# Scores of attention group 0 in one piece over four PSUM banks, with later transposes and a later exchange of maxima

## The chip, the cores and the metric

The kernel runs on one core of a Trainium2 chip. The core has five engines with a queue each, and every engine works through its own queue strictly in the order in which the program issued to it: PE (TensorE, matrix products), DVE (VectorE), ACT (ScalarE), POOL (GpSimd) and SP (SyncE, which here only issues DMAs). Engines wait for each other through semaphores. PE writes its products to PSUM, which has eight banks of 128 x 512 fp32; a bank that still holds something to be read can't be written by the next product. The metric is the time of one execution on the device in microseconds (us).

## The reference

Two residual layers over a sequence of 512 rows of 1024 numbers, all in fp32. Layer 0 mixes tokens by attention over three groups (dilations 1, 4, 16), layer 1 by a short gated convolution; a squared-ReLU MLP follows each of them. The change concerns the attention only, cut here to what matters:

```python
def mixer_a(h, w_qkv, q_gain, k_gain, w_o, cos, sin):
    qkv = (h @ w_qkv).reshape(B, S, A_GROUPS, 3, A_HEADS, HEAD_DIM)      # 3 groups x (q, k, v) x 16 heads x 64
    for g in range(A_GROUPS):
        q = partial_rope(rms_norm(qkv[:, :, g, 0], q_gain[g]), cos, sin)
        k = partial_rope(rms_norm(qkv[:, :, g, 1], k_gain[g]), cos, sin)
        num, den, mx = dilated_group(q, k, qkv[:, :, g, 2], dil, radius) # scores, row max, exp, sums, scores @ v
    wts = jnp.exp(mx - jnp.max(mx, axis=0, keepdims=True))               # the groups are joined by their maxima
    num = jnp.sum(wts[..., None] * jnp.stack(nums, 0), axis=0)
    den = jnp.sum(wts * jnp.stack(dens, 0), axis=0)
    return (num / den[..., None]).reshape(B, S, D_MODEL) @ w_o
```

## The kernel before

Each fp32 factor is split into a high and a low part (`split`, L285: ACT casts the high part at L288, the low part is a subtraction at L289, by POOL for the weights), and each product is made of three PE matmuls: high by high, high by low, low by high.

**Units, blocks and groups.** The attention goes by pairs of heads, p = 0 to 7. A pair has three units of projections: A (q and k of group 0, q of group 1), B (k of group 1, q and k of group 2) and V (the values of all groups). A unit multiplies 8 weight tiles (a tile is one k of 128 rows) with 4 blocks r of 128 rows of the sequence, in 96 matmuls of 384 columns at L128, into the 4 banks of the pool psG, one bank for each r. It is cut into 4 blocks of 24 matmuls with 2 weight tiles each (pair 0's first unit into 8). Positions are counted in "groups" of 16 such matmuls, so a block is 1.5 groups long, one matmul is 0.0625 group and a pair is 18 groups. In a block the matmuls go by r, so a unit's first matmul needs the bank of r = 0 and its seventh that of r = 1. When a bank's last matmul is through, it is emptied: unit A by `evacA`, unit B by `evacB` (L320), unit V by `evacV` (L327), which casts the values with ACT at L291 and subtracts with DVE at L292. Only then can the next unit's matmuls write to that bank.

**The order written by hand.** Between the matmuls of the units stand the tasks of the attention. `PLACES` (L60) gives each task a position in groups after the end of unit A (for A's tasks) or unit B (for all others); its first entry is for pair 0, the second for pairs 1 to 6, the third for pair 7. `attn_tasks` (L587) puts them on a heap, and the loop at the end of the kernel runs a task when the matmul that reaches its position has been issued. Before the first matmul of each block the same loop calls `prep_to` and `load_to`, which prepare the two weight tiles of the block two blocks further on (ACT's cast and POOL's subtraction) and issue the DMAs of later tiles. There are 6 buffers for prepared tiles (wh and wl) and 4 for raw ones (wraw): a raw buffer is loaded again when POOL's subtraction L289 has read it, and SP, which issues the loads (L567, or L725 for the output weights), waits for that.

**The attention tasks of a pair** that the change and the prediction touch, with their places for pairs 1 to 6, in groups after the end of unit B, so within unit V:

- sqB (0.17 to 0.92): the four squares of the rows of B (ACT L361) and their sums (DVE L362); rsB (0.97): the reciprocal root in eleven small DVE instructions (L365, L151 to L157); mulB (1.07 to 1.43): scaling (DVE L371) and rotation (L376, L378), three of the four blocks on POOL.
- S0: the scores of group 0. `S0(bp)` does two of the four blocks b of queries. Each needs 3 matmuls for each of 2 heads, 64 rows of the array by 256 columns (L443), the two heads side by side on the two halves of the array. A call takes two banks of the pool psT (3 banks, tile "st"), and DVE then adds the mask and takes the row maximum, four times (L447). The first call stands at 0.45, the second at 1.0.
- E0: eight exponentials on ACT (L466), four from 1.1 and four from 1.65, in steps of 0.15.
- TA and TB, the transposes (`qk_fill`, L380): four PE transposes (L387) bring a q or k into a bank of psT, ACT scales and casts it (L401), DVE takes the low part (L403). TB fills k1, q2 and k2 at 4.05, 4.24 and 4.43. A fill of k1 or k2 is two instructions on ACT and two on DVE, one for each head.
- X1 (3.1) and X2 (5.3): the exchange of maxima; a spread on DVE (L424), eight small matmuls (L433) and a copy (L478).
- S12, E12, W, N12, N0 from 6.5 on: scores of groups 1 and 2, weights and normalization; then PT and PV: PT transposes the scores, PV multiplies them with the values into the one bank of the pool psO (tile "o"). The last PV of a head is followed by ACT's copy (L547) and DVE's sum (L548), which empty that bank. Pair 0's last PV stands at 0.61 of pair 1's counting, that of the other pairs at -0.12 of the next pair's.

After pair 7 follow the output projection (its first unit uses three of psG's banks), the MLP, the convolution and the second MLP, none of which the change touches.

Of the kernel before, what the change touches and what calls it, by code (L numbers as in the profile page):

```python
# [11 lines left out]
F32 = mybir.dt.float32  # L12
# [23 lines left out]
def _constants():  # L36
# [10 lines left out]
    for n, b in enumerate((0, 1, 3)):  # L47
# [11 lines left out]

PLACES = [  # L60
    dict(sqA=0.52, rsA=0.95, mulA=2.62, dmA=0.05, TA=7.6, dT=0.25, sqB=0.08, rsB=1.22, mulB=2.1, dmB=0.1, TB=6.2, S0=2.6,
         dS=1.0, E0=3.75, X=5.5, lX=2.0, S12=8.1, dS12=0.3, E12=8.7, dE12=0.2, W=10.3, lW=0.35, lF=0.9, N0=11.65, N12=10.75,
         dN=0.04, P=12.45, dP=0.58, gP=0.5, lP=1.6, qA=0, qB=0, pA=0, pB=3, pN=2, vA=0, vB=0, xq=2.7, dxq=0.3, xs=5.35,
         lg=2.48, dlg=0.36, tb=4.6, dtb=0.15, gc=6.7),
    dict(sqA=0.02, rsA=0.87, mulA=1.79, dmA=0.28, TA=4.8, dT=0.19, sqB=0.17, rsB=0.8, mulB=1.07, dmB=0.12, TB=4.05, S0=0.45,
         dS=0.55, E0=1.1, X=3.1, lX=2.2, S12=6.5, dS12=0.24, E12=7.1, dE12=0.2, W=8.9, lW=0.35, lF=0.9, N0=10.25, N12=9.4,
         dN=0.04, P=10.9, dP=0.64, gP=0.9, lP=1.6, qA=0, qB=0, pA=0, pB=3, pN=2, vA=0, vB=12),
    dict(sqA=0.02, rsA=0.87, mulA=1.79, dmA=0.28, TA=4.8, dT=0.19, sqB=0.17, rsB=0.8, mulB=1.07, dmB=0.12, TB=4.05, S0=0.45,
         dS=0.55, E0=1.1, X=3.1, lX=2.8, S12=6.8, dS12=0.24, E12=7.4, dE12=0.2, W=9.2, lW=0.4, lF=1.0, N0=10.7, N12=9.75,
         dN=0.04, P=12.0, dP=0.5, gP=0.45, lP=1.2, qA=0, qB=0, pA=0, pB=3, pN=2, vA=0, vB=9),  # L70
]

# [2 lines left out]
def trunk_kernel(ctx, tc, x, norm1, norm2, wqkv, qgain, kgain, wo, win, conv, wout, w1, w2, c_rope, c_m0, c_m12, out):  # L75
    nc = tc.nc
    pe, act, dve, pool, sync = nc.tensor, nc.scalar, nc.vector, nc.gpsimd, nc.sync
    ctx.enter_context(tc.manual_schedule())

    def ptile(p, shape, dt, name, **kw):  # L80
        return p.tile(shape, dt, name=name, **kw)
# [323 lines left out]
    def q0v(t, h, b):  # L405
        return t[64 * h:64 * h + 64, 128 * b:128 * b + 128]
# [26 lines left out]
            pe.matmul(ps[32 * b:32 * b + 32, :n], fold, t[:, n * b:n * b + n], start=True, stop=True)  # L433
        return ps[:, :n].rearrange("p (a j) -> p j a", a=4)

    def S0(bp):
        ps = [ptile(psT, [128, 512], F32, "st") for _ in range(2)]
        (qh, ql), (kh, kl) = qk["q0"], qk["k0"]
        for b2 in range(2):
            b = 2 * bp + b2  # L440
            for q, (a, k) in enumerate(((qh, kh), (qh, kl), (ql, kh))):
                for h in range(2):
                    pe.matmul(ps[h][:, 256 * b2:256 * b2 + 256], q0v(a, h, b), k0v(k, h, b), start=(q == 0), stop=(q == 2))  # L443
        for h in range(2):
            for b2 in range(2):
                b = 2 * bp + b2
                dve.tensor_tensor_reduce(out=sm0[:, h, b], in0=ps[h][:, 256 * b2:256 * b2 + 256],  # L447
                                         in1=msk0[:, (0, 1, 1, 2)[b]], scale=1.0, scalar=3.0e38, op0=ALU.add, op1=ALU.min,
                                         accum_out=mx(N0)[:, 4 * h + b:4 * h + b + 1])

# [136 lines left out]
    def attn_tasks(p, tA, tB, c):  # L587


        tS = tB  # L590

        def put(pos, name, fn, *needs):
            def go():
                for n in needs:
                    need(*n)
                fn()
                mark(name, p)
            at(pos, go)

        for r in range(4):  # L600
            put(tA + c["sqA"] + 0.25 * r, "sqA", lambda r=r: norm_sq(rawA, stA, 6, r, r < c["qA"]), ("evA", p, 4))
        put(tA + c["sqA"] + c["rsA"], "rsA", lambda: norm_rs(stA, 6), ("sqA", p, 4), ("stats", 0, 1))
        for r in range(4):
            put(tA + c["mulA"] + c["dmA"] * r, "mulA", lambda r=r: norm_mul(rawA, stA, 6, tabA, r, pool if r < c["pA"] else dve), ("rsA", p, 1), ("tables", 0, 6))
        for i, nm in enumerate(("q0", "k0", "q1")):
            put(tA + c["TA"] + c["dT"] * i, "TA", lambda i=i, nm=nm: qk_fill(rawA, i, nm, i), ("mulA", p, 4), ("cols", 0, 1),
                ("S0", p - 1, 2), ("S12", p - 1, 4))
        for r in range(4):
            put(tB + c["sqB"] + 0.25 * r, "sqB", lambda r=r: norm_sq(rawB, stB, 6, r, r < c["qB"]), ("evB", p, 4))
        put(tB + c["sqB"] + c["rsB"], "rsB", lambda: norm_rs(stB, 6), ("sqB", p, 4))  # L610
        for r in range(4):
            put(tB + c["mulB"] + c["dmB"] * r, "mulB", lambda r=r: norm_mul(rawB, stB, 6, tabB, r, pool if r < c["pB"] else dve), ("rsB", p, 1))
        for i, nm in enumerate(("k1", "q2", "k2")):
            put(tB + c["TB"] + c["dT"] * i, "TB", lambda i=i, nm=nm: qk_fill(rawB, i, nm, 3 + i), ("mulB", p, 4),
                ("S12", p - 1, 4))
        for i in range(2):
            put(tS + c["S0"] + c["dS"] * i, "S0", lambda i=i: S0(i), ("TA", p, 3), ("PT", p - 1, 8), ("gains", 0, 11))
            for n in range(4):
                put(tS + c["E0"] + c["dS"] * i + 0.15 * n, "E0", lambda i=i, n=n: exps(0, n // 2, 2 * i + n % 2), ("S0", p, i + 1))

        def sp0():
            st[p]["sp0"] = spread(mx(N0, 2), 16)

        put(tS + c["X"], "X1", sp0, ("E0", p, 8), ("perm", 0, 1))
        put(tS + c["X"] + c["lX"], "X2", lambda: stats_over(p), ("X1", p, 1), ("N0", p - 1, 8))
        for r in range(4):
            put(tS + c["S12"] + c["dS12"] * r, "S12", lambda r=r: S12(r), ("TB", p, 3), ("PT", p - 1, 8))
            for h in range(2):
                put(tS + c["E12"] + c["dE12"] * (2 * r + h), "E12", lambda h=h, r=r: exps(1, h, r), ("S12", p, r + 1))
        w = tS + c["W"]  # L630
        put(w, "W1", weigh1, ("E12", p, 8), ("X2", p, 1))
        put(w + 0.1, "W2", weigh2, ("W1", p, 1))
        put(w + c["lW"], "W3", lambda: weigh3(p), ("W2", p, 1))
        put(w + c["lW"] + c["lF"], "W4", lambda: weights_back(p), ("W3", p, 1))
        for n in range(8):
            put(tS + c["N12"] + c["dN"] * n, "N12", lambda n=n: pnorm(1, n // 4, n % 4, n % 4 >= c["pN"]), ("W3", p, 1))
            put(tS + c["N0"] + c["dN"] * n, "N0", lambda n=n: pnorm(0, n // 4, n % 4, n % 4 >= c["pN"]), ("W4", p, 1))
        for n, (h, i) in enumerate([(h, i) for h in range(2) for i in range(4)]):
            s = tS + c["P"] + c["dP"] * n + c["gP"] * (n > 3)
            put(s, "PT", lambda h=h, i=i: PT(p, h, i), ("N12" if i > 1 else "N0", p, 8))  # L640
            put(s + c["lP"], "PV", lambda h=h, i=i, n=n: PV(p, h, i, n % 4 == 0, n % 4 == 3), ("PT", p, n + 1), ("evV", p, 4),
                ("v0", p, 8))
# [3 lines left out]
    c = PLACES[0]  # L646
# [370 lines left out]
```

## Time and profile before

| | |
|---|---|
| Median of the three runs | 1487.7 us (1486.6 to 1487.86) |
| The profiled execution, on the device | 1487.62 us |
| Its span, first to last instruction | 1485.8 us |
| Mean granted TensorE clock | 0.997 |
| PE: share of the span with a matmul running | 99% |
| DVE, ACT, POOL | 48%, 45%, 47% |
| One steady pair, from one first S0 call to the next (190.87 to 258.09 us) | 67.2 us |
| L443, all 192 matmuls of S0, sum of their durations | 31.1 us |

The profile lists, for each engine, when its instructions ran, and for idle time what ended it. Consecutive matmuls overlap in the records, because each has a latency longer than the step from one to the next. So the table's 99% says that PE hardly ever stands empty, and the pace has to be read from the distance between starts. An instruction that waits holds up everything behind it in its engine's queue, whatever that is for.

### The profile page before, as it was taken

What the parts mean: (1) busy time and instruction counts of PE and PEld (TensorE: products, weight loads), DVE (VectorE), ACT (ScalarE), POOL (GpSimd) and SP (SyncE); (2) the same over time, 40 slices, a digit from 0 to 9 for tenths busy, and PEclk for the clock granted to TensorE, in tenths of its full rate; (3) what the DMA queues carried; (4) which work ended last, traced back from release to release, by engine and by line L of the source; (5) the groups of instructions that cost most, each with busy time, mean ns of one, the idle gap of its engine ahead of it and who ended that gap; (6) DMA issues with size and microseconds to landing.
All of it is one profiled execution on the core that took longest, in us unless ns stands there. A gap on an engine that the chain in (4) does not pass through costs nothing.

```text
span 1485.8 us, 22525 instructions
## 1 busy us (share of the span) xinstructions
PE 1474.2 (99%) x7900; PEld 1291.2 (87%) x7900; DVE 708.0 (48%) x1460; ACT 663.2 (45%) x1359; POOL 702.9 (47%) x671
## 2 busy tenths in 40 slices
PE   9899999999999999999999999999999999999998
PEld 8899999999999998888888888878888888888887
DVE  6777667676767684822021223554447330122222
ACT  5456565656556573544342332433343443333320
POOL 4444444536454444455444445444455554544442
PEclk9999999999999999999999999999999999999999
DMA  6432322323132323232222222233332222222222
GB/s 170 132 104 69 94 87 78 102 65 115 54 115 67 101 98 130 96 113 93 95 97 99 99 97 95 82 89 93 100 113 100 99 93 92 100 99 96 99 89 85
DMA packets 164509, 144.76 MB, mean 97 GB/s; under 512 B 13812, under 2 KB 125484, under 8 KB 164396
## 3 DMA queue, kind: packets, MB, share of 16 engines
q1 hardware_dynamic: 164076, 143.06, 30.7%
q8 instruction: 62, 1.02, 0.3%
q14 instruction: 51, 0.42, 0.1%
q10 hardware_dynamic: 320, 0.27, 0.1%
HBM read 134.89 MB, written 8.39 MB: 96 GB/s over the span
## 4 chain that ended last, share of the span: by engine, by line
PE 93%; DVE 3%; issue 1%; ACT 1%; DMA 1%; SPq 1%; POOL 0%; DVEq 0%; POOLq 0%; ACTq 0%
PE g L128 85%; PE o L544 3%; PE st L516 2%; PE st L457 2%; PE st L387 1%; PE st L443 1%; DMA sm<-in_x 0%; POOL wl L289 0%; DVE sm L504 0%; SPq L567 0%; ACT sqx L273 0%; PE g L873 0%; DMA wraw<-in_a_wqkv 0%; ACT wh L288 0%; PE st L433 0%
## 5 line engine op out<-in xcount | busy, mean ns | idle before, releaser
L289 POOL TENSOR_TENSOR wl<-wraw,wh 128x512 fp32r<-128x512 f32 (+1 forms) x544 | 636.9, 1192 | 702.6 <-ACT wh L288 688.3
L288 ACT CAST wh<-wraw 128x512 fp32r<-128x512 f32 (+1 forms) x544 | 300.3, 569 | 500.0 <-PE g L128 376.2
L128 PE MATMUL g<-hgBh,wl 128*128 128x512 f32 x704 | 274.3, 390 | 0.5 <-POOL wl L289 0.4
L128 PE MATMUL g<-hgBh,wh 128*128 128x512 f32 x704 | 274.0, 389 | 0.1
L128 PE MATMUL g<-hgBl,wh 128*128 128x512 f32 x704 | 273.9, 389 | 0.0
L128 PE MATMUL g<-wh,hgl 128*128 128x384 f32 x768 | 268.2, 349 | 0.3 <-DVE hgl L302 0.2
L128 PE MATMUL g<-wl,hgh 128*128 128x384 f32 x768 | 262.4, 342 | 0.0
L128 PE MATMUL g<-wh,hgh 128*128 128x384 f32 x768 | 262.0, 341 | 0.0
L805 DVE SCALAR_TENSOR_TENSOR zr<-g,R 128x512 f32<-128x512 f32 x64 | 44.0, 691 | 283.2 <-PE g L128 283.0
L128 PEld LDWEIGHTS g<-hgBh,wl 128*128 128x128 f32 x704 | 132.2, 188 | 29.6 <-POOL wl L289 2.2
L128 PEld LDWEIGHTS g<-hgBh,wh 128*128 128x128 f32 x704 | 132.2, 188 | 27.8 <-ACT wh L288 0.5
L128 PEld LDWEIGHTS g<-hgBl,wh 128*128 128x128 f32 x704 | 132.2, 188 | 27.3
L128 PEld LDWEIGHTS g<-wh,hgl 128*128 128x128 f32 x768 | 145.2, 189 | 3.3 <-DVE hgl L302 1.2
L128 PEld LDWEIGHTS g<-wh,hgh 128*128 128x128 f32 x768 | 145.5, 189 | 0.3 <-issue 0.2
L128 PEld LDWEIGHTS g<-wl,hgh 128*128 128x128 f32 x768 | 145.1, 189 | 0.4
L822 DVE TENSOR_TENSOR acc<-g,acc 128x512 f32<-128x512 f32 x32 | 22.1, 692 | 138.2 <-PE g L128 138.2
L128 PE MATMUL g<-z0h,wh 128*128 128x512 f32 x192 | 74.7, 389 | 0.0
L128 PE MATMUL g<-z0l,wh 128*128 128x512 f32 x192 | 74.7, 389 | 0.0
L128 PE MATMUL g<-z0h,wl 128*128 128x512 f32 x192 | 74.7, 389 | 0.0
L466 ACT ACTIVATE sm<-sm,mxs 128x256 f32<-128x256 f32 x128 | 63.9, 501 | 15.5 <-DVE mxs L460 12.2
L288 ACT CAST pth<-st 128x512 fp32r<-128x512 f32 x64 | 37.5, 585 | 65.4 <-PE st L516 63.0
L806 ACT ACTIVATE zz<-zr 128x512 f32<-128x512 f32 x64 | 40.5, 633 | 38.7 <-DVE zr L805 36.8
(212 smaller groups left out, 2354.4 us busy)
## 6 DMA issues: line engine op xcount, KB each, us to landing
wraw<-in_mlp_w SPq DMA_DIRECT2D x256, 256.0 KB
wraw<-in_a_wqkv SPq DMA_DIRECT2D x128, 128.0 KB
wraw<-in_a_wqkv SPq DMA_DIRECT2D x64, 192.0 KB
wraw<-in_a_wqkv SPq DMA_DIRECT2D x128, 64.0 KB
wraw<-in_b_win SPq DMA_DIRECT2D x64, 128.0 KB
v0d<-v SPq DMA_DIRECT2D x8, 512.0 KB
v<-v0d SPq DMA_DIRECT2D x64, 64.0 KB
wraw<-in_b_win SPq DMA_DIRECT2D x64, 64.0 KB
```

Of the source, the lines that this page charges most:

```text
L128: pe.matmul(unit["ps"][n][:, :width], a, b, start=st, stop=sp)
L288: act.copy(hi, src)
L289: (eng or dve).tensor_sub(lo, src, f32(hi))
L387: pe.transpose(o, raw[r][:, w, :], ident)
L443: pe.matmul(ps[h][:, 256 * b2:256 * b2 + 256], q0v(a, h, b), k0v(k, h, b), start=(q == 0), stop=(q == 2))
L457: pe.matmul(pv[:, :, g], a[:, 128 * r:128 * r + 128], k[:, 256 * r:256 * r + 256], start=(q == 0), stop=(q == 2))
L466: act.activation(t[:, h, b], t[:, h, b], AF.Exp, bias=mx(m)[:, c], scale=-1.0, accum_out=mx(d)[:, c])
L516: pe.transpose(ps[:, 128 * n:128 * n + 128], src, ident)
L544: pe.matmul(out_, stat, mov, start=first and q == 0, stop=last and q == len(ops) - 1, skip_group_check=True)
L805: dve.scalar_tensor_tensor(zr, ps, 0.0, state["R"], op0=ALU.max, op1=ALU.mult)
L806: after(0.4, lambda: act.activation(zz, zr, AF.Square))
L822: dve.tensor_add(a, ps, a)
```

## The change

`S0` becomes one call for all four blocks of queries. It takes three banks of psT and the one bank of psO, issues its 24 matmuls in a row, and then the eight maxima, now by block and then by head. In `PLACES`:

- S0 stands at 0.75 for pairs 1 to 7 (the two calls stood at 0.45 and 1.0); for pair 0 at 2.6 (they stood at 2.6 and 3.6).
- The eight exponentials E0 go by block and then by head, from 1.35 in steps of 0.18 (pair 0: from 3.5).
- TB goes from 4.05 to 4.25 for pairs 1 to 7; its step of 0.19 stays, so the three fills stand at 4.25, 4.44 and 4.63.
- X goes from 3.1 to 3.25 for pairs 1 to 7. Both X1 and X2 move with it.

A need is added: S0 asks that all eight PV of the pair before have been issued, because it now uses their bank.

```diff
-         dS=1.0, E0=3.75, X=5.5, ...
+         dS=0.18, E0=3.5, X=5.5, ...
...
-    dict(... TB=4.05, S0=0.45,
-         dS=0.55, E0=1.1, X=3.1, ...
+    dict(... TB=4.25, S0=0.75,
+         dS=0.18, E0=1.35, X=3.25, ...
...
-    def S0(bp):
-        ps = [ptile(psT, [128, 512], F32, "st") for _ in range(2)]
+    def S0():
+        ps = [[ptile(psT, [128, 512], F32, "st"), ptile(psT, [128, 512], F32, "st")],
+              [ptile(psT, [128, 512], F32, "st"), ptile(psO, [128, 512], F32, "o")]]
         (qh, ql), (kh, kl) = qk["q0"], qk["k0"]
-        for b2 in range(2):
-            b = 2 * bp + b2
+        for b in range(4):
             for q, (a, k) in enumerate(((qh, kh), (qh, kl), (ql, kh))):
                 for h in range(2):
-                    pe.matmul(ps[h][:, 256 * b2:256 * b2 + 256], q0v(a, h, b), k0v(k, h, b), start=(q == 0), stop=(q == 2))
-        for h in range(2):
-            for b2 in range(2):
-                b = 2 * bp + b2
-                dve.tensor_tensor_reduce(out=sm0[:, h, b], in0=ps[h][:, 256 * b2:256 * b2 + 256],
+                    pe.matmul(ps[b // 2][h][:, 256 * (b % 2):256 * (b % 2) + 256], q0v(a, h, b), k0v(k, h, b), start=(q == 0),
+                              stop=(q == 2))
+        for b in range(4):
+            for h in range(2):
+                dve.tensor_tensor_reduce(out=sm0[:, h, b], in0=ps[b // 2][h][:, 256 * (b % 2):256 * (b % 2) + 256],
                                          in1=msk0[:, (0, 1, 1, 2)[b]], ...
...
-        for i in range(2):
-            put(tS + c["S0"] + c["dS"] * i, "S0", lambda i=i: S0(i), ("TA", p, 3), ("PT", p - 1, 8), ("gains", 0, 11))
-            for n in range(4):
-                put(tS + c["E0"] + c["dS"] * i + 0.15 * n, "E0", lambda i=i, n=n: exps(0, n // 2, 2 * i + n % 2), ("S0", p, i + 1))
+        put(tS + c["S0"], "S0", S0, ("TA", p, 3), ("PT", p - 1, 8), ("PV", p - 1, 8), ("gains", 0, 11))
+        for n in range(8):
+            put(tS + c["E0"] + c["dS"] * n, "E0", lambda n=n: exps(0, n % 2, n // 2), ("S0", p, 1))
```

More of the change, by code (lines that the diff above doesn't have):

```diff
@@ L61 @@
     dict(sqA=0.52, rsA=0.95, mulA=2.62, dmA=0.05, TA=7.6, dT=0.25, sqB=0.08, rsB=1.22, mulB=2.1, dmB=0.1, TB=6.2, S0=2.6,
-         dS=1.0, E0=3.75, X=5.5, lX=2.0, S12=8.1, dS12=0.3, E12=8.7, dE12=0.2, W=10.3, lW=0.35, lF=0.9, N0=11.65, N12=10.75,
+         dS=0.18, E0=3.5, X=5.5, lX=2.0, S12=8.1, dS12=0.3, E12=8.7, dE12=0.2, W=10.3, lW=0.35, lF=0.9, N0=11.65, N12=10.75,
          dN=0.04, P=12.45, dP=0.58, gP=0.5, lP=1.6, qA=0, qB=0, pA=0, pB=3, pN=2, vA=0, vB=0, xq=2.7, dxq=0.3, xs=5.35,
          lg=2.48, dlg=0.36, tb=4.6, dtb=0.15, gc=6.7),
-    dict(sqA=0.02, rsA=0.87, mulA=1.79, dmA=0.28, TA=4.8, dT=0.19, sqB=0.17, rsB=0.8, mulB=1.07, dmB=0.12, TB=4.05, S0=0.45,
-         dS=0.55, E0=1.1, X=3.1, lX=2.2, S12=6.5, dS12=0.24, E12=7.1, dE12=0.2, W=8.9, lW=0.35, lF=0.9, N0=10.25, N12=9.4,
+    dict(sqA=0.02, rsA=0.87, mulA=1.79, dmA=0.28, TA=4.8, dT=0.19, sqB=0.17, rsB=0.8, mulB=1.07, dmB=0.12, TB=4.25, S0=0.75,
+         dS=0.18, E0=1.35, X=3.25, lX=2.2, S12=6.5, dS12=0.24, E12=7.1, dE12=0.2, W=8.9, lW=0.35, lF=0.9, N0=10.25, N12=9.4,
          dN=0.04, P=10.9, dP=0.64, gP=0.9, lP=1.6, qA=0, qB=0, pA=0, pB=3, pN=2, vA=0, vB=12),
-    dict(sqA=0.02, rsA=0.87, mulA=1.79, dmA=0.28, TA=4.8, dT=0.19, sqB=0.17, rsB=0.8, mulB=1.07, dmB=0.12, TB=4.05, S0=0.45,
-         dS=0.55, E0=1.1, X=3.1, lX=2.8, S12=6.8, dS12=0.24, E12=7.4, dE12=0.2, W=9.2, lW=0.4, lF=1.0, N0=10.7, N12=9.75,
+    dict(sqA=0.02, rsA=0.87, mulA=1.79, dmA=0.28, TA=4.8, dT=0.19, sqB=0.17, rsB=0.8, mulB=1.07, dmB=0.12, TB=4.25, S0=0.75,
+         dS=0.18, E0=1.35, X=3.25, lX=2.8, S12=6.8, dS12=0.24, E12=7.4, dE12=0.2, W=9.2, lW=0.4, lF=1.0, N0=10.7, N12=9.75,
          dN=0.04, P=12.0, dP=0.5, gP=0.45, lP=1.2, qA=0, qB=0, pA=0, pB=3, pN=2, vA=0, vB=9),
@@ L606, in attn_tasks @@
             put(tA + c["TA"] + c["dT"] * i, "TA", lambda i=i, nm=nm: qk_fill(rawA, i, nm, i), ("mulA", p, 4), ("cols", 0, 1),
-                ("S0", p - 1, 2), ("S12", p - 1, 4))
+                ("S0", p - 1, 1), ("S12", p - 1, 4))
         for r in range(4):
```

## Prediction

> **What bounds the kernel now.** The page comes first. It has the span, to which the rest is held, and PE's share of it.
>
> ```profile
> span 1485.8 us, 22525 instructions
> PE 1474.2 (99%) x7900; PEld 1291.2 (87%) x7900; DVE 708.0 (48%) x1460; ACT 663.2 (45%) x1359; POOL 702.9 (47%) x671
> ```
>
> PE runs a matmul nearly all the time, so time is won or lost in two ways only: by the pace of the matmuls, or by a new wait of PE. Next, what PE waits for at all, longest first:
>
> ```profile
> PE st L443 <- DVE q0l L403: 2.9, 1, 2.9
> ```
>
> Its longest wait is one of 2.9 us in pair 0. No row of that view shows PE waiting in every pair, so in pairs 1 to 6 only the pace counts. The timeline of PE around S0 in a steady pair (pair 3) shows it (start, duration, engine, line):
>
> ```profile
> 258.02 0.39 PE L443 MATMUL st<-k0h,q0h 64*128 64x256 f32 x2
> 258.24 0.28 PE L443 MATMUL st<-k0l,q0h 64*128 64x256 f32 x2
> ...
> 258.71 0.28 PE L443 MATMUL st<-k0h,q0l 64*128 64x256 f32 x2
> ...
> 259.20 0.34 PE L128 MATMUL g<-wh,hgh 128*128 128x384 f32 x1
> ...
> 260.42 0.34 PE L128 MATMUL g<-wl,hgh 128*128 128x384 f32 x1
> 260.68 0.39 PE L443 MATMUL st<-k0h,q0h 64*128 64x256 f32 x2
> ```
>
> Read the distances between starts. The matmuls of unit V follow each other at (260.42 - 259.20) / 7 = 0.174 us; the pairs of S0 (two heads side by side) at (258.71 - 258.24) / 4 = 0.118 us. From the first call's start to the second's are 2.66 us, for nine matmuls of V (1.57) and six pairs (0.71). The rest, 0.39 us, is the price of one change of PE from 128 rows to two halves of 64 rows and back.
>
> **What the change removes.** Two such changes a pair become one: 8 x 0.39 = 3.1 us less. In pair 0, S0 still begins behind the same DVE instruction, so one change goes there too. This is all that the change can win, since the count of matmuls, maxima, exponentials and transposes stays.
>
> **What it moves: the chain from DVE to TB.** S0 goes from behind the 8th matmul of its block to behind the 13th. DVE's queue in the same pair:
>
> ```profile
> 259.29 0.41 DVE L447 CUSTOM_DVE_ANT_0 sm<-st,msk 128x256 f32<-128x256 f32 x1
> ...
> 260.67 1.01 DVE L362 TENSOR_REDUCE stB<-sqq 128x6 f32<-128x384 f32 x2
> ...
> 265.60 2.58 DVE L371 TENSOR_TENSOR rawB<-rawB,stB 128x384 f32<-128x384 f32 x4
> ...
> 274.32 1.50 DVE L403 SCALAR_TENSOR_TENSOR k2l<-st,cols,k2h 64x512 fp32r<-64x512 f32 x2
> 275.86 1.14 DVE L292 SCALAR_TENSOR_TENSOR v<-g,small,v 128x384 fp32r<-128x384 f32 x2
> ```
>
> Up to 265.60 DVE works without a gap: two sums of squares end as the first row begins, then four maxima (1.38 us), two sums (0.50 each), the reciprocal root from 261.68 to 264.22 (265.60 less four more maxima), the second four. The new order is: two sums, the third, all eight maxima, the fourth, the root, mulB (265.60). The third sum needs its square from ACT:
>
> ```profile
> 258.95 0.98 ACT L361 ACTIVATE sqq<-rawB 128x384 f32<-128x384 f32 x2 [0.21 <-DVE stB L362]
> ```
>
> The first of these two squares ends at 259.44. So: third sum 259.48 to 259.98, eight maxima 2.76 to 262.74, fourth sum to 263.24, root 2.54 to 265.78. mulB starts 0.2 us later. POOL's rotation hangs on that, and on POOL the weights' subtractions queue behind it:
>
> ```profile
> POOL tmpRP L376 <- DVE rawB L371: 54.1, 8, 9.1
> ```
>
> ```profile
> 270.11 3.92 POOL L289 TENSOR_TENSOR wl<-wraw,wh 128x384 fp32r<-128x384 f32 x4
> ```
>
> Eight times, once a pair, POOL stands idle until mulB's first step. Then come the rotations and the four subtractions, of which the second ends at 270.11 + 1.96 = 272.07. It frees the raw buffer of a weight tile, and SP's queue shows the next load issued at that moment:
>
> ```profile
> 272.13 1.36 SPq L567 DMA_DIRECT2D wraw<-in_a_wqkv  x3
> ```
>
> This tile is cast by ACT at the start of V's last block (4.5 groups), two blocks after its buffer was asked for. How long a load takes from issue to landing is shown where the chain of waits runs through one, in pair 7 (there also for a tile of 128 x 384 fp32):
>
> ```profile
> 541.84 2.45 DMA wraw<-in_a_wo
> ```
>
> I take 2.45 us. So the tile lands at 272.13 + 2.45 = 274.58 before, and 274.78 after. Now ACT's queue:
>
> ```profile
> 270.69 1.39 ACT L401 ACTIVATE k1h<-st,cols 64x512 fp32r<-64x512 f32 x2 [2.86 <-PE st L387]
> 272.10 0.69 ACT L401 ACTIVATE q2h<-st,cols 128x512 fp32r<-128x512 f32 x1
> 272.69 1.37 ACT L401 ACTIVATE k2h<-st,cols 64x512 fp32r<-64x512 f32 x2
> 274.08 1.06 ACT L288 CAST wh<-wraw 128x384 fp32r<-128x384 f32 x2
> 275.17 1.73 ACT L291 ACTIVATE v<-g,small 128x384 fp32r<-128x384 f32 x3
> ```
>
> Before, the three fills of TB stand at 4.05, 4.24 and 4.43, all ahead of the two weight casts of the block at 4.5. The second cast starts at 274.08 + 0.53 = 274.61, just when the tile has landed. In pair 5 it does wait a little:
>
> ```profile
> 409.25 0.51 ACT L288 CAST wh<-wraw 128x384 fp32r<-128x384 f32 x1 [0.18 <-DMA wraw<-in_a_wqkv]
> ```
>
> After, k2 stands at 4.63: its fill is issued after the block at 4.5 has begun, so **the two casts of the weights now stand ahead of k2's fill on ACT**, and behind k2's fill the first cast of the values. ACT would wait for a DMA, which by itself costs nothing as the weights are needed two blocks later, but k2 and the values queue behind it, and the values hold the banks of psG. When PE wants them, and when it wants TB:
>
> ```profile
> 270.02 0.63 PE L387 MATMUL st<-ident,rawB 128*128 128x128 f32 x4
> ```
>
> ```profile
> 277.15 0.34 PE L128 MATMUL g<-wh,hgh 128*128 128x384 f32 x1
> ```
>
> The steps, in pair 3's time:
>
> - PE: the first fill goes from behind the block's 17th matmul to behind its 21st, 0.70 us, less the 0.39 saved: 270.33. The last rotation, which it needs, ends 0.2 later than before and so just in time. Unit V ends 0.39 earlier, and the first matmul of the next unit is wanted at 277.15 - 0.39 = 276.76.
> - ACT: k1 from 271.0, q2 done by 273.0, then the casts. The second waits for the landing at 274.78 and ends at 275.3. k2 takes 1.37, to 276.7.
> - DVE: the second half of k2's low part (half of 1.50) follows k2's cast and ends at 277.45; meanwhile ACT casts the first block of the values (0.58). Its subtraction (half of 1.14) ends at 278.0. Before, it ended at 275.86 + 0.57 = 276.43, 0.7 us before PE needed the bank.
> - With about 0.1 us for the handovers PE goes on at 278.1. It has waited 1.35 us where it waited for nothing, and is 278.1 - 277.15 = **0.95 us later** than before in this pair, the saving counted. The second bank is wanted six matmuls (1.04 us) later and its subtraction ends 0.6 us after the first: no further wait.
>
> Six pairs (1 to 6): +5.7 us. In pair 7 PE already waits here, and resumes when the same chain lets it:
>
> ```profile
> 546.70 1.43 PE g L128 x5
> ```
>
> After, the load lands 0.2 later, at 544.5, and the casts end at 545.1; then k2 (1.37), the half of its low part (0.75) and the subtraction (0.6), which before were not in the chain or ran beside it: PE resumes at 547.9, +1.2 us. The later chain of pair 7 hangs on PE's place and shifts with it.
>
> **The rest.** S0's fourth bank is psO's. In pairs 2 to 7 the last PV stands 0.87 group ahead of S0, with fourteen matmuls of V between. In pair 1 it is three:
>
> ```profile
> 124.88 0.58 ACT L547 COPY tmpO<-o 64x512 f32<-64x512 f32 x1 [2.94 <-PE o L544]
> ```
>
> ```profile
> 125.49 0.69 DVE L548 TENSOR_TENSOR oT<-o,tmpO 64x512 f32<-64x512 f32 x1 [0.42 <-ACT tmpO L547]
> ```
>
> The bank is free 1.30 us after PV's end (to 126.18). S0 asks for it after three matmuls of V (0.5), a change of rows and six pairs (0.9): about 1.4 us after PV. Price 0 to 0.3 us, once; I take 0.15. The exponentials end at most 0.4 us later, covered by the 2.86 us for which ACT idles before k1; without that cover they would push TB one for one. X2's matmuls move by three places, and the copy behind them stays behind the second block of the values on DVE: nothing. Three banks of psT taken at once instead of two: TB asks for them again over 10 us after S0: nothing. SP isn't passed by anything; its loads come 0.2 us later as counted.
>
> **The sum.** -0.4 (pair 0) + 5.7 (pairs 1 to 6) + 1.2 (pair 7) + 0.15 = +6.7 us. On the profiled execution (span 1485.8, 1487.62 on the device) this is 1492.5 and 1494.3; its time is within 0.1 of the runs' median, so the prediction is 1487.7 + 6.7 = **1494.4 us**. Bounds: if landings are 0.2 longer, as pair 5's wait hints, +8.1; if the change of rows is not saved besides, 3.1 more, +11.2. Below, nothing in the rows bounds a landing, so the range reaches to the case without a net loss.
>
> **The rivals.**
>
> *The wait is covered, and only the saving remains (faster).* Place: the first matmul of the next unit. PE wants the bank at 276.76, so the chain must be 1.35 us shorter: the second tile would have to land 1.1 us after its issue. Then 8 x 0.39 stand: 1484.6 us. For it: PE's queue shows no wait here in any of pairs 1 to 6, and 0.7 us of slack. Against it: the 2.45 us, and pair 5, where the cast waited for the landing even behind k2. Chance 0.09.
>
> *Wait and saving cancel.* A landing near 1.5 us after issue, or k2's fill elsewhere in ACT's queue by half of what I work out, gives about 1487.7 us. For it: most casts before began at once, so the landing may be earlier than 274.58. Chance 0.11.
>
> *The waits slow TensorE's clock.* In pair 0 the 2.9 us of waiting were followed by a low granted clock (the figure behind the five busy times):
>
> ```profile
> 59.00:66.00 7.00, 6.72 (x28) 6.04 (x28) 5.56 (x17) 2.77 (x9) 4.88 (x7) 0.57 0.01 2
> ```
>
> That is 7 us at 0.57, so 3.0 us lost on top of the wait. A wait of 0.76 us was not; the clock of the microsecond around it is 1.00:
>
> ```profile
> 52.15 0.33 PE L387 MATMUL st<-ident,rawA 128*128 128x128 f32 x1 [0.76 <-DVE rawA L378]
> ```
>
> ```profile
> 52.00:53.00 1.00, 0.85 (x5) 0.84 (x6) 1.00 (x3) 0.41 (x1) 0.00 (x0) 1.00 0.85 245
> ```
>
> My 1.35 us lie between. If each of the seven waits cost 3.0 more: +21, 1515 us; a single one, 1497. The shorter row is the nearer one, so chance 0.08.
>
> The Trainium skill, in "TensorE: Matmul & The Clock Gate" (section "Part 1: The HAM clock gate"), has the clock drop only after an idle window of about 3.4 us. By that rule a 1.35 us wait costs no clock and the sum stays as it is, but the rule is not exact here: 2.9 us were enough in this trace.
>
> **How the numbers follow.** The forecast (PE waits at the start of each next unit) has the remaining 0.72, with an own range of 1491 to 1499. The range 1486.5 to 1499 adds the case that cancels, and leaves out the gain, the clock and little else, under 2 in 10. A measurement of this kernel tells 0.2% (3.0 us) from no change, so faster means below 1484.7 and slower above 1490.7. The gain lies on the lower edge and is split: faster 0.05; same 0.04 + 0.11 = 0.15; slower 0.80.
>
> **What would show it.** In the changed kernel's timeline one S0 of 24 matmuls, with one change of rows; ACT's order k1, q2, two weight casts, k2, the second cast ended by a DMA; PE waiting over 1 us for DVE L292 at the first matmul after each unit V of pairs 1 to 7, and a steady pair of about 68.2 us. I am wrong if the casts start without waiting, if PE doesn't wait for L292, or if the clock's row falls outside pair 0.

## The result, and the profile after

The changed kernel takes 1507.4 us (median of 4 runs, 1506.78 to 1508.33), the kernel before on the same chip 1487.78 us (4 runs, 1486.6 to 1488.16). The ratio is 1.0134 with a 95% interval of [1.0121, 1.0147]: 19.6 us slower, where 6.7 were forecast and 11.3 was the upper end of the range. The mechanism of the forecast is there, at the place that it named, but it costs twice as much per pair, and the clock, which was given a chance of 0.08, joins in.

First the head of the page of after, and what PE waits for (total, times, longest):

```profile
span 1505.0 us, 22518 instructions
PE 1478.6 (98%) x7900; PEld 1296.0 (86%) x7900; DVE 709.3 (47%) x1460; ACT 659.2 (44%) x1359; POOL 703.2 (47%) x671
```

```profile
PE g L128 <- DVE v L292: 14.4, 7, 2.7
```

This row is new: in each of pairs 1 to 7 PE waits for the values' subtraction, in all 14.4 us. PE's timeline of pairs 2 to 4 (start, duration, engine, line; lines after S0 are one higher than before the change):

```profile
262.86 0.39 PE L444 MATMUL st<-k0h,q0h 64*128 64x256 f32 x2
...
332.05 0.39 PE L444 MATMUL st<-k0h,q0h 64*128 64x256 f32 x2
...
333.67 0.44 PE L128 MATMUL g<-wl,hgh 128*128 128x384 f32 x1
...
343.66 0.60 PE L387 MATMUL st<-ident,rawB 128*128 128x128 f32 x4
...
349.89 0.34 PE L128 MATMUL g<-wh,hgl 128*128 128x384 f32 x1
352.20 0.44 PE L128 MATMUL g<-wh,hgh 128*128 128x384 f32 x1 [1.96 <-DVE v L292]
352.47 0.34 PE L128 MATMUL g<-wl,hgh 128*128 128x384 f32 x1
...
352.82 0.51 PE L128 MATMUL g<-wh,hgh 128*128 128x384 f32 x1
353.13 0.52 PE L128 MATMUL g<-wl,hgh 128*128 128x384 f32 x1
...
402.83 0.39 PE L444 MATMUL st<-k0h,q0h 64*128 64x256 f32 x2
```

S0 is one piece now. Unit V's last matmul starts at 349.89 and the next unit's first 2.31 us later; the profile counts 1.96 us of that as idle. Shortly after, the step between matmuls goes from 0.174 to 0.32 us. Pair 3, from S0 to S0, takes 69.19 us (262.86 to 332.05) and pair 4 takes 70.78 (332.05 to 402.83), against 67.23 before (the mean of pairs 2 to 6). What differs between them is the clock. Here are the 5.7 to 6 us after each of the seven waits; the figure behind the five busy times is the granted clock:

```profile
143.20:149.00 5.80, 5.80 (x40) 5.80 (x41) 3.73 (x16) 1.53 (x6) 1.99 (x2) 1.00 0.50 159
212.30:218.00 5.70, 5.70 (x28) 5.70 (x29) 2.71 (x11) 1.58 (x6) 1.98 (x2) 0.70 0.34 100
283.00:289.00 6.00, 6.00 (x41) 6.00 (x42) 3.89 (x16) 1.63 (x6) 1.99 (x2) 1.00 0.48 152
352.30:358.00 5.70, 5.70 (x28) 5.70 (x29) 2.71 (x11) 1.57 (x6) 1.97 (x2) 0.70 0.50 160
423.00:429.00 6.00, 6.00 (x41) 6.00 (x42) 3.86 (x16) 1.61 (x6) 1.99 (x2) 1.00 0.57 178
492.20:498.00 5.80, 5.80 (x29) 5.80 (x30) 2.82 (x11) 1.56 (x6) 1.98 (x2) 0.71 0.33 100
564.00:570.00 6.00, 6.00 (x30) 4.82 (x31) 2.36 (x9) 1.91 (x5) 1.97 (x2) 0.72 0.51 164
```

After the waits of pairs 2, 4, 6 and 7 the mean clock of these stretches is 0.70 to 0.72, after the others it is full. A pair with the low clock is about 1.55 us longer than its neighbour. Behind the mean stands a short stretch at half the clock. The trace records each change of the granted clock: behind these four waits it falls to 0.50 for 3.41 us each time, and it does so at 212.87, 352.82, 492.77 and 564.45 us, whole multiples of 3.413 us apart (41, 41 and 21). Cut at the borders of such steps, the waits of pair 3 (two rows) and pair 4 (two rows) look like this (the first busy time is PE's, the figure behind the five the clock again):

```profile
281.14:284.56 3.42, 1.61 (x9) 1.61 (x10) 3.37 (x7) 2.40 (x6) 1.36 (x2) 1.00 0.27 78
284.56:287.97 3.41, 3.41 (x27) 3.41 (x26) 1.56 (x8) 1.10 (x4) 0.63 (x1) 1.00 0.58 179
349.41:352.82 3.41, 1.45 (x8) 1.13 (x7) 2.80 (x6) 3.34 (x7) 0.93 (x2) 1.00 0.45 129
352.82:356.23 3.41, 3.41 (x14) 3.41 (x14) 0.97 (x2) 0.00 (x0) 1.59 (x2) 0.50 0.31 85
```

Pair 3's wait begins 0.10 us ahead of a border and leaves 1.81 us idle in the step behind it; pair 4's lies in one step with all its 1.96 us. The last section comes back to this.

Now the engines that PE waits for. ACT in pair 4:

```profile
344.30 1.38 ACT L401 ACTIVATE k1h<-st,cols 64x512 fp32r<-64x512 f32 x2 [3.55 <-PE st L387]
345.70 0.69 ACT L401 ACTIVATE q2h<-st,cols 128x512 fp32r<-128x512 f32 x1
347.38 0.52 ACT L288 CAST wh<-wraw 128x384 fp32r<-128x384 f32 x1 [0.98 <-DMA wraw<-in_a_wqkv]
348.15 0.51 ACT L288 CAST wh<-wraw 128x384 fp32r<-128x384 f32 x1 [0.25 <-DMA wraw<-in_a_wqkv]
348.57 1.37 ACT L401 ACTIVATE k2h<-st,cols 64x512 fp32r<-64x512 f32 x2
349.97 1.99 ACT L291 ACTIVATE v<-g,small 128x384 fp32r<-128x384 f32 x4
```

And DVE:

```profile
349.98 1.51 DVE L403 SCALAR_TENSOR_TENSOR k2l<-st,cols,k2h 64x512 fp32r<-64x512 f32 x2 [1.97 <-ACT k2h L401]
351.52 1.14 DVE L292 SCALAR_TENSOR_TENSOR v<-g,small,v 128x384 fp32r<-128x384 f32 x2
```

ACT's order is the one forecast: k1, q2, the two weight casts, k2, the values. Both casts begin when a DMA lands (1.23 us of waiting), and k2 waits behind them though its own data are there. The new thing is in DVE's first row. It begins at 349.98, after **both** parts of k2h (348.57 + 1.37 = 349.94), so k2l's two parts run wholly behind k2h, not beside it. The values' first subtraction ends half of 1.14 after 351.52, at 352.09, and PE goes on at 352.20.

Summed over the span (19.2 us longer): pairs 1 to 6, from S0 to S0, cost 15.7 us. S0 itself stands five matmuls (0.87 us) later in its unit; with that taken out, pair 7 and what follows cost 4.3, and pair 0 and the start gain 0.8.

### The profile page after: what moved, and what is told of

It is laid out like the page before. It is cut to its first block, busy times and chain, and to the rows that moved or that the text cites. A ratio compares the mean times of both kernels' runs of the same rounds, so it can differ in the third digit from the quotient of the medians.

```text
span 1505.0 us, 22518 instructions
## 1 busy us (share of the span) xinstructions
PE 1478.6 (98%) x7900; PEld 1296.0 (86%) x7900; DVE 709.3 (47%) x1460; ACT 659.2 (44%) x1359; POOL 703.2 (47%) x671
## 4 chain that ended last, share of the span: by engine, by line
PE 82%; issue 7%; POOL 3%; DVE 3%; ACT 2%; DMA 2%; SPq 1%; POOLq 0%; ACTq 0%; DVEq 0%
PE g L128 76%; PE o L545 2%; PE st L517 2%; POOL wl L289 2%; PE st L458 2%; DMA wraw<-in_a_wqkv 1%; POOL tmpRP L376 1%; ACT v L291 1%; ACT k2h L401 1%; SPq L568 1%; POOL rawB L378 0%; PE st L387 0%; ACT wh L288 0%; DMA sm<-in_x 0%; DVE v L292 0%
## 5 line engine op out<-in xcount | busy, mean ns | idle before, releaser
L128 PE MATMUL g<-wh,hgh 128*128 128x384 f32 x768 | 265.8, 346 | 11.7 <-DVE v L292 11.7
L128 PEld LDWEIGHTS g<-wh,hgh 128*128 128x128 f32 x768 | 145.6, 190 | 14.3 <-DVE v L292 13.6
```

The costliest lines, as they stand in the source:

```text
L128: pe.matmul(unit["ps"][n][:, :width], a, b, start=st, stop=sp)
```

## The experiments

My theory: the place of TB alone makes the loss, since it puts k2 behind the weight casts; the length of the waits decides whether the clock adds to it. Rivals: S0's one piece is the cost (its four banks, its longer row of maxima); or the landing of the weights is late whatever ACT's order. Each kernel is compared with runs of the kernel before on its chip, whose medians lay between 1487.07 and 1487.93 us.

### TB's place alone (e2_tb_alone)

The kernel before, with TB at 4.25, nothing else:

```diff
-  TB=4.05, S0=0.45,
+  TB=4.25, S0=0.45,
```

> The kernel before with only TB moved from 4.05 to 4.25 for pairs 1 to 7; S0 stays in two calls at its old places, E0 and X too. Theory (order on ACT): k2's fill is behind the two weight casts here as well, so PE waits for DVE L292 at the start of each next unit, 1.4 to 1.9 us in pairs 1 to 6 and about 2.3 in pair 7 (a little less than in the changed kernel, as V doesn't end 0.39 us earlier and mulB isn't later): +11 us without low clocks, up to +17 with four of them, 1498 to 1505 us. Rival A (the piece itself): no wait, 1487 to 1488.5 us.

Measured: 1501.73 us (1499.86 to 1502.77), ratio 1.0093 [1.0076, 1.0110]. What PE waits for in this kernel:

```profile
PE g L128 <- DVE v L292: 11.4, 7, 2.4
```

The move of TB alone gives 14.3 of the 19.6 us, with S0 still in two pieces, so the piece isn't needed for the loss. Its waits are 1.4 to 1.7 us in pairs 1 to 6, and none of those six is followed by a low clock; pair 7's (2.4 us) is. What the other edits add, 5.3 us, isn't a cost of their own (the next two kernels have them without it): with them V's last matmul comes a little earlier (20.20 us after V's first, against 20.42) and the chain ends a little later (the next unit starts at 22.45 against 22.2), so the wait grows to 1.9 or 2.2 us, and now the clock falls after half of the waits.

### k2 ahead of the casts (e1_k2_ahead), and the casts behind k2 (e3_casts_later)

Two ways of undoing only ACT's order, the rest of the change kept. In the first, the three fills stand closer together, at 4.25, 4.37 and 4.49, so that k2 is issued before the block at 4.5:

```diff
-  put(tB + c["TB"] + c["dT"] * i, "TB", ...)
+  put(tB + c["TB"] + c.get("dTB", c["dT"]) * i, "TB", ...)      # dTB=0.12 for pairs 1 to 7
```

> The changed kernel with one place altered: TB's step is 0.12 instead of 0.19 for pairs 1 to 7, so the three fills stand at 4.25, 4.37 and 4.49, and k2's fill is issued before the two weight casts of the block at 4.5 instead of behind them. Theory (order on ACT): k2 no longer waits for a weight's DMA, PE's seven waits for DVE L292 (2.0 us each in the changed kernel) shrink to 0 to 0.2 us, no low clock after them, and the saved changes of rows stand: 1484.5 to 1486.5 us. Rival A (the piece itself): the eight maxima in a row, DVE's later mulB and the bank of psO cause the wait; then the waits stay near 2 us and the time between 1500 and 1507.

In the second, TB stays as changed, and the weights of V's last block are prepared four matmuls into it, behind k2:

```diff
-        prep_to(...); load_to(...)                # ahead of the block
+        if not late: prepare()
+        ...
+            if late and q == 3: prepare()         # late: V's last block, pairs 1 to 7
```

> The changed kernel with TB where the change puts it (4.25, 4.44, 4.63), but the preparation of two weight tiles that belongs to the start of V's last block is issued four matmuls into that block, behind k2's fill (pairs 1 to 7). Theory (order on ACT): the same as with k2 ahead of the casts, since only the order of the two decides: 1484.5 to 1487 us, waits of PE for DVE L292 of 0 to 0.3 us. Rival B (k2 is late by its own place, and the casts don't matter): waits and time stay as in the changed kernel, 1503 to 1508 us. Rival A: 1500 to 1507 us.

Measured: 1487.45 us, ratio 1.0000 [0.9990, 1.0009], and 1487.83 us, ratio 1.0004 [0.9995, 1.0014]. ACT in the first kernel, same pair:

```profile
338.37 1.38 ACT L401 ACTIVATE k1h<-st,cols 64x512 fp32r<-64x512 f32 x2 [3.55 <-PE st L387]
339.78 0.69 ACT L401 ACTIVATE q2h<-st,cols 128x512 fp32r<-128x512 f32 x1
340.36 1.36 ACT L401 ACTIVATE k2h<-st,cols 64x512 fp32r<-64x512 f32 x2
341.75 0.94 ACT L288 CAST wh<-wraw 128x384 fp32r<-128x384 f32 x2
```

k2 goes first, the casts find their tiles landed, and the whole loss of 19.6 us is gone, although the last fill moved by only 0.14 group (0.4 us). So the order in ACT's queue is the cause, not the landing. But both kernels miss the other half of their expectation: the saving of 3.1 us doesn't appear. Their steady pairs take 67.18 and 67.20 us against 67.23. Set matmul by matmul against the kernel before, pair 4 of the first kernel is 0.38 us ahead right behind S0, 0.23 at V's end and 0.05 eight matmuls into the next unit. The last step, 0.18 us, is what is left of the same wait. PE's rows show no idle time there, but its weight load (PEld) does:

```profile
344.21 0.19 PEld L128 LDWEIGHTS g<-wh,hgh 128*128 128x128 f32 x1 [0.23 <-DVE v L292]
```

So undoing the order leaves the chain just long enough to end last. The other 0.15 us is lost in V itself, and the later experiments look for it.

### Cast and low part by turns (e4_interleave)

If DVE starts on k2's low part only after both casts because the program issues both casts first, issuing them by turns should let DVE begin 0.7 us earlier:

```diff
         for h_, l_, v, sc in parts:
             act.activation(h_, v, AF.Copy, scale=sc)
-        for h_, l_, v, sc in parts:
             dve.scalar_tensor_tensor(l_, v, sc, f32(h_), ...)
```

> The changed kernel with one order altered inside a fill: for k0, k1 and k2, which are two instructions each on ACT and on DVE, ACT's first part is followed by DVE's first part and then by the second parts, so that DVE can take the first low part while ACT casts the second half. In the changed kernel DVE starts the first low part of k2 only when both casts are done, which the prediction had missed (0.75 us a pair). Theory: PE's waits for DVE L292 shrink by 0.75 us to 1.3 us, 7 x 0.75 = 5.3 us less; if the low clock that followed four of the seven waits needs waits near 2 us, it goes too, another 6 us less: 1496 us, or 1502 us if it stays. Rival (the low parts aren't on the path): 1506 to 1508 us.

Measured: 1510.15 us, ratio 1.0154 [1.0139, 1.0169], slower still: the expectation failed. ACT in pair 4 of this kernel (its line numbers after `qk_fill` are one lower):

```profile
346.87 0.68 ACT L401 ACTIVATE k1h<-st,cols 64x512 fp32r<-64x512 f32 x1 [3.55 <-PE st L387]
348.37 0.69 ACT L401 ACTIVATE k1h<-st,cols 64x512 fp32r<-64x512 f32 x1 [0.81 <-DVE k1l L402]
...
351.18 0.68 ACT L401 ACTIVATE k2h<-st,cols 64x512 fp32r<-64x512 f32 x1
352.68 0.68 ACT L401 ACTIVATE k2h<-st,cols 64x512 fp32r<-64x512 f32 x1 [0.81 <-DVE k2l L402]
```

Now ACT's second part waits until DVE has read the first. The two parts lie in different halves of one tile of k, but a common tile alone doesn't make the engines take turns: ACT casts the values without a gap from 349.97 to 351.96 (above), while DVE subtracts in the same tile v from 351.52 on. There each block of values has a PSUM bank of its own. The parts of a fill are read by both engines from one bank, st. Two instructions at the kernel's start share only this, a cast by ACT and a copy by DVE that doesn't read the cast's result:

```profile
11.38 0.68 ACT L300 ACTIVATE hgh<-st,cols 128x512 fp32r<-128x512 f32 x1
12.10 0.69 DVE L301 COPY oT<-st 128x512 f32<-128x512 f32 x1 [2.47 <-ACT hgh L300]
```

The copy begins 0.04 us after the cast, and so it is in 7 of 8 such pairs of the changed kernel and in all 8 of the kernel before (in the other one it begins later still). So this program's waits keep ACT and DVE from reading one bank st at the same time, and casts and low parts never overlap within a fill, whichever order the program has; here ACT stands still in between as well. No run gives the two parts a bank each.

### A longer wait (e8_tb_later)

```diff
-  TB=4.25, S0=0.75,
+  TB=4.4, S0=0.75,
```

> The changed kernel with the transposes 0.15 group later still (4.4): q2 as well as k2 now stands behind the two casts on ACT, 0.69 us more ahead of V's evacuation, so the wait of every pair should be 2.9 us instead of 2.25. Theory (length of the wait decides whether TensorE's clock falls: 2.9 us always, 2.25 every other time, 2.0 never): low clock after all seven waits, 7 x 0.65 for the waits and 3 x 1.55 for the clock over the changed kernel: 1514 to 1519. Rival (low clock after every other wait whatever its length): 1510.5 to 1513.5. Rival (q2 doesn't lengthen the wait): 1506 to 1509.

Measured: 1517.68 us, ratio 1.0204 [1.0190, 1.0218]. The waits are 2.5 to 3.2 us by the profile's count of idle time. The microseconds behind the first two:

```profile
146.50:152.00 5.50, 5.50 (x38) 5.50 (x39) 3.43 (x15) 1.53 (x6) 1.99 (x2) 1.00 0.50 159
216.50:222.00 5.50, 5.50 (x27) 5.50 (x28) 2.52 (x9) 1.55 (x6) 1.98 (x2) 0.69 0.37 112
```

The clock is low (0.66 to 0.72) after six of the seven. That is not quite the "all" of the theory, and more than the half of its rival; the time lies where the theory had it. A longer wait makes the fall likelier, and another 0.15 group costs another 10 us. The wait without a fall (the first, 2.76 us) lies across a border of the 3.413 us steps, with 1.80 us in one step and 0.96 in the next.

### Where the saving went: S0's place (e5_tb_back, e6_phase, e7_s0_late)

TB put back to 4.05, S0 still in one piece at 0.75:

```diff
-  TB=4.25, S0=0.75,
+  TB=4.05, S0=0.75,
```

> The changed kernel with the second half's transposes put back to 4.05; S0 stays in one piece at 0.75 and the exchange of maxima at 3.25. Theory (the transposes' place alone makes the 2 us waits; the piece is nearly neutral): k2's two parts stand ahead of the casts on ACT again, no wait for DVE's v over 0.3 us. In the run with k2 ahead of the casts the first transpose of the second half stood at 337.74 us and GpSimd's rawB had ended at 337.70, so four matmuls earlier (0.69 us) TensorE must wait for GpSimd 0.5 to 0.7 us per pair, at the transposes. Six or seven pairs of +0.5 less the 0.04 that the piece saved: 1489.5 to 1492. Rival (the piece is itself the cost, by its four banks and longer row of maxima): over 1495. Rival (the piece is worth the forecast 3.1): 1485 or less.

Measured: 1490.27 us, ratio 1.0019 [1.0010, 1.0027]. PE's longest wait in it:

```profile
PE st L387 <- POOL rawB L378: 3.0, 7, 0.7
```

This is the wait for which the change had moved TB: with the eight maxima (2.8 us in a row on DVE) ahead of the norm, POOL's last rotation comes later than the first transpose. The pair takes 67.57 us, 0.57 of it more than usual at the transposes. Without that it would be 67.00, so the piece itself saves 0.23 us, not 0.39.

Part of the difference is the pace behind S0. In the changed kernel the 56 matmuls from S0 to TB take 343.66 - 333.67 = 9.99 us (0.178 each, the slower first step included). Before, 48 took 8.43 us from this row to the TB row of 270.02 (0.176):

```profile
261.59 0.44 PE L128 MATMUL g<-wh,hgl 128*128 128x384 f32 x1
```

Without the first step, it is 0.1767 against 0.1734. I took the cause to be the matmul into which S0 returns:

```diff
-  dTB=0.12, S0=0.75,
+  dTB=0.12, S0=0.68,
```

> The kernel with k2 ahead of the casts (1487.45 against 1487.46), with S0 two matmuls earlier (0.68 for 0.75). Theory: what the piece saves on the change of rows was given back by a slower pitch of L128's matmuls behind it, 0.1767 us against 0.1733, over 53 matmuls of every pair. In both kernels the pitch holds from S0 to the next excursion of TensorE, and S0 returns into a matmul of wl in the one and of wh with the low part in the other; two matmuls earlier it returns into the latter, as before the change. If that sets the pitch: 0.173 to 0.174 in the 53 matmuls and 0.16 to 0.18 us less per pair, 1486.0 to 1486.7. Rival (the pitch comes from the data or from the one long piece, not from the place of the return): 0.1765 to 0.177 again, 1487.2 to 1487.7.

Measured: 1488.01 us, ratio 1.0003 [0.9994, 1.0012], step 0.1768, steady pair 67.20 us (the profiled execution waits 1.37 us for the values in pair 1 besides). That idea falls; the slow step goes with the one piece.

Then S0 behind the norm, to take the maxima off POOL's way:

```diff
-  TB=4.25, S0=0.75, ... E0=1.35
+  TB=4.05, S0=1.57, ... E0=1.9
```

> The changed kernel with S0 in one piece behind the second half's norm instead of ahead of it (1.57 for 0.75, exps at 1.9), and the transposes at 4.05 as before the change. Theory: DVE's eight maxima (0.35 us each, 2.8 us in a row) stood ahead of the norm's chain that GpSimd's rawB and with it the transposes wait for; behind it, rawB is ready about 2.8 us earlier, k2 goes ahead of the casts, and neither the wait for GpSimd nor that for DVE's v is left. S0 returns into wh with the low part, so the pitch is 0.1735 as well. Then the whole forecast saving of the piece appears: 0.35 to 0.39 us per pair, 1484.5 to 1485.2. Rival (something else takes it back): 1486.5 to 1488. Slower than 1489 if the exchange of maxima at 3.25 comes too early for the late maxima.

Measured: 1494.36 us, ratio 1.0045 [1.0031, 1.0059]. The saving doesn't show, and the loss isn't the exchange of maxima. The wait for POOL is gone, but ACT has a new one to pass on:

```profile
339.68 0.51 ACT L467 ACTIVATE sm<-sm,mxs 128x256 f32<-128x256 f32 x1
...
340.31 1.38 ACT L401 ACTIVATE k1h<-st,cols 64x512 fp32r<-64x512 f32 x2
```

TB's first transpose stands at 337.99, but the eight exponentials, late because the maxima are late, with two weight casts ahead of the last, keep ACT until 340.3, and k1 queues behind them. PE waits about 0.9 us a pair for the values (7.6 us in all, 2.3 of it in pair 7), once more through ACT's queue.

### S0 in the middle of the norm (e9_s0_mid), and the slow step (e10_o_first, e11_h_swap)

S0 between the second and the third row of mulB, so that POOL can start on two rows:

```diff
-  TB=4.25, S0=0.75, ... E0=1.35
+  TB=4.05, S0=1.2,  ... E0=1.56
```

> S0 in one piece between the second and the third row of the second half's norm (1.2 for 0.75, exps from 1.56), transposes at 4.05 as before the change. With S0 ahead of the norm and the transposes at 4.05 TensorE waited 0.57 us a pair at the transposes for GpSimd's rawB; with S0 behind the norm the exps stood on ACT ahead of k1 and TensorE waited 1.22 us a pair for DVE's v. Theory (the row of eight maxima on DVE, 2.8 us, is what must not stand ahead of GpSimd's three rows nor so late that the exps delay k1): in the middle, GpSimd starts two of its rows ahead of the maxima and ends 0.8 us earlier, and the exps are over before k1; both waits go. Period of a pair 66.9 to 67.1 us against 67.24 before the change, 1485.0 to 1486.5. Rival (one of the two waits stays, 0.3 us or more a pair): 1487 to 1490.

Measured: 1487.38 us, ratio 0.9996 [0.9987, 1.0005]. The steady pair takes 66.99 us as expected, but the time isn't down: pair 7, which has the low parts of the output projection on DVE as well, now waits 1.84 us for the values and has the low clock behind that: its next unit starts 2.18 us after V's last matmul, where it was 0.57 before. On top of this kernel, two tries at the slow step, the bank and the heads:

```diff
-  ps = [[st, st], [st, o]]
+  ps = [[o, st], [st, st]]
```

> The kernel with S0 in the middle of the norm, and the one bank from the pool of o taken by S0's first matmuls instead of its last. L128's pitch after S0 in one piece was 0.1766 in four kernels, whatever matmul it returned into, and 0.1733 after S0 in two pieces. If the pitch comes from the bank that S0's last matmuls write (o's in all four, st's before the change): 0.1733 here, and 0.14 us less per pair than its neighbour with o last (45 matmuls x 0.0033), 1 us in all. If it comes from the length of the piece: 0.1766 again and the same time within 0.4 us.

```diff
-  for h in range(2): pe.matmul(ps[b // 2][h]...)
+  for h in (1, 0): pe.matmul(ps[b // 2][h]...)
```

> The kernel with S0 in the middle of the norm, and the two heads of S0 in the other order, so that its last matmul uses the first 64 rows of TensorE and not the last 64. If the pitch of L128 behind S0 hangs on the rows used last: 0.1733 and 0.14 us less per pair. If on the length of the piece, or on anything else that this leaves alone: 0.1766 and the same time within 0.4 us.

Measured: 1487.07 us, ratio 0.9999 [0.9990, 1.0008], and 1486.68 us, ratio 0.9994 [0.9985, 1.0003]. PE in pair 4, first with S0 in the middle (e9), then with the heads swapped besides (e11); both rows are 45 matmuls of V apart:

```profile
327.22 0.44 PE L128 MATMUL g<-wh,hgl 128*128 128x384 f32 x1
...
335.27 0.60 PE L387 MATMUL st<-ident,rawB 128*128 128x128 f32 x4
```

```profile
326.23 0.45 PE L128 MATMUL g<-wh,hgl 128*128 128x384 f32 x1
...
334.15 0.60 PE L387 MATMUL st<-ident,rawB 128*128 128x128 f32 x4
```

8.05 us against 7.92. The bank changes nothing (8.05 too, steady pair 66.99); the order of the heads does (steady pair 66.88). With it, one S0 saves 0.35 us a pair, nearly the forecast 0.39.

### Both together (e12_best)

Pairs 1 to 6 as in e11, pair 7 as in e1:

```diff
-  TB=4.05, S0=1.2,  ... E0=1.56      # pair 7
+  TB=4.25, dTB=0.12, S0=0.75, ... E0=1.35
```

> Pairs 1 to 6 as in the kernel with the heads swapped and S0 in the middle of the norm (66.88 us a pair against 67.24 before the change); the last pair as in the kernel with k2 ahead of the casts (S0 at 0.75, the transposes at 4.25, 4.37 and 4.49), since with S0 in the middle its wait for DVE's v was 2.2 us against 0.57 before and it was followed by a low clock. Theory: 6 x 0.36 less, the last pair within 0.5 us of before, the first 0.3 less: 1484.5 to 1485.7. Rival (the last pair's wait wasn't what held the swapped kernel at 1486.7): 1486.2 or more.

Measured: 1484.66 us (1482.44 to 1486.18, 11 runs) against 1487.93, ratio 0.9981 [0.9972, 0.9990]: faster than both kernels, and than the one before by 3.3 us (1.5 to 4.2), or 0.2%. Its span, PE's wait for the values, and one steady pair (66.87 us):

```profile
span 1482.3 us, 22505 instructions
```

```profile
PE g L128 <- DVE v L292: 0.6, 1, 0.6
```

```profile
391.26 0.39 PE L444 MATMUL st<-k0h,q0h 64*128 64x256 f32 x2
...
458.13 0.39 PE L444 MATMUL st<-k0h,q0h 64*128 64x256 f32 x2
```

Between the two traces pairs 1 to 6 give 2.4 us. From pair 7 on 0.6 us is lost, and 1.7 us is gained ahead of pair 1: 0.7 at the start, and 1.0 in pair 0, where the low clock lasted one step of 3.41 us and in the kernel before two. How much of that last part the edits bring isn't shown.

## Why the prediction was wrong

The direction, the place and the cause were right; the sum was too small by a factor of three. Step by step:

- **The order on ACT, the landing, the casts: right.** k1, q2, two casts that begin with a landing, then k2. The two kernels that undo only this order are rid of the whole 19.6 us.
- **DVE's part of the chain: the step that failed.** "The second half of k2's low part (half of 1.50) follows k2's cast" let DVE do the first half beside ACT's second. It does neither half before both casts are over, and the experiment with turns and the rows beside it show why: both engines read the two halves from one bank, and they take turns there. That is 0.75 us in each of seven pairs. The trace of before had it, in a row that I didn't read against ACT's:

```profile
272.11 1.51 DVE L403 SCALAR_TENSOR_TENSOR k1l<-st,cols,k1h 64x512 fp32r<-64x512 f32 x2 [2.34 <-ACT k1h L401]
```

  k1h's two parts end at 270.69 + 1.39 = 272.08, and only then does k1l begin. With 0.75 more, the forecast net loss of 0.95 us is 1.70 a pair.
- **The saving by one piece, 0.39 us: about 0.2 of it came.** S0 in one piece as the change has it is followed by matmuls that are 0.003 us slower, 0.15 to 0.18 us a pair. With that the loss is 1.87; the pair without low clock measures 69.19 - 67.23 = 1.96.
- **The clock: dismissed too cheaply.** The rival "each of the seven waits costs 3.0 more" had the waits at 1.35 us, nearer to the one of 0.76 that cost nothing. At 1.9 to 2.7 us, four of seven fell, at about 1.55 each: 6.2 us. The rival was right in kind and wrong in size: its 7 us at 0.57 in pair 0 were two steps of 3.41 us at half the clock, and behind these waits it was one. The rule of the Trainium skill that I weighed against it ("TensorE: Matmul & The Clock Gate", section "Part 1: The HAM clock gate", an idle window of about 3.4 us) doesn't hold here: the clock was low after an idle time of 1.84 us. That only four fell was the luck of where the waits lay among the steps of 3.413 us, which nothing in the prediction set.
- **Together:** pairs 1 to 6: 6 x (0.95 + 0.75 + 0.16) = 11.2, and three low clocks 4.7, are 15.9, measured 15.7. Pair 7: 1.2 + 0.75 + 1.55 = 3.5, measured with the rest 4.3. Most of the remaining 0.8 us isn't of the wait: the kernels with k2 ahead of the casts and with the casts behind k2 lose 0.6 and 0.7 us from pair 7 on, without the long wait and the low clock.
- **Pair 0 and the bank of psO:** the 0.15 us in pair 1 came: S0, from its first matmul to the next of V, takes 1.77 us there and 1.62 in every later pair, and its matmuls into tile o start late. Pair 0 and the start are 0.8 us less than before where 0.4 less was forecast. This is neither borne out nor refuted: the start moves by more than that from one execution to the next, and pair 0's low clock lasted 6.83 us before and 3.41 after.
- **What would show it:** the one S0, ACT's order, the cast that a DMA ends and the wait for L292 were there; the pair of 68.2 us was not, and the clock's row outside pair 0, named as a sign of being wrong, came.

Open is how the order of the heads slows the matmuls behind S0 (0.1766 against 0.1736 us). That it does is shown by one edit, and the last kernel has it too; why, no run here shows. That two pieces in the old order had the fast step speaks against the rows used last as the whole answer.

## What to carry to other kernels

When a task is moved past a place where the program issues other work, write down the new order of every engine's queue, and look for an instruction in it that begins when a DMA lands: all that queues behind it inherits that wait, and a later place by 0.14 group made the difference between 0 and 19.6 us here. Read from the trace whether two engines really work on two halves at the same time, above all where both read them from one PSUM bank, before letting them overlap in a sum. And price a new wait of TensorE not only by its length: from 1.84 us on, a slow clock behind it could cost 1.55 us more here, depending on where it fell.

## What the runs showed of the hardware

- The clock after a wait of PE. By the length of the wait alone (the profile's idle time, pairs 1 to 7 of the changed kernel and the experiments): at 1.7 us and less (six waits of e2, six of e7 at about 0.9 us, one of 1.37 in e6) the clock never fell; from 1.8 to 2.2 us it fell after 9 of 15 (3 of 6 in after and 3 of 6 in e4, in both after every other wait, and all three of e9 to e11 in pair 7); from 2.3 to 3.2 us after 10 of 11.
- What decides besides the length is the place. In each trace the changes of the granted clock lie whole multiples of 3.413 us apart, within 0.003 us, and each fall behind one of these waits lasts one such step at 0.50, with about half the pace (0.32 us a matmul for 0.174). Take for each of the 39 waits the step in which PE was idle longest. With up to 1.82 us idle in it (18 waits) the clock never fell; from 1.87 us on (17 waits) it always fell in the next step; of the four in between two fell. So a wait of 2.76 us that lay across a border cost no clock (1.80 and 0.96 us), and one of 1.84 us inside a step did. It also gives the every-other pattern: two pairs of the changed kernel, one with and one without the fall, take 139.9 us, nearly 41 steps (139.95), so each wait lies about half a step from the one before.
- The Trainium skill ("TensorE: Matmul & The Clock Gate", section "Part 1: The HAM clock gate") calls the window free-running, by which a wait's place in the window would decide. The traces agree: the steps keep their distance through the whole run, and lie differently against the first instruction in each.
- One change of PE from 128 rows to two halves of 64 and back costs 0.35 to 0.39 us in this kernel, and the order of the two halves within it can change the step of the matmuls that follow, by 0.003 us in 0.174, until the next such change.
